# Retention states in a hybrid encoder layer: one 128x128 product per chunk, or one 64x64 product per head in the array's column halves

## The chip, the cores and the metric

The kernel runs on one core of a Trainium2 chip. The metric is the time of one execution on the device in microseconds; each kernel is run several times, and the median is taken. The engines of the core work side by side, each in the order of its own instructions: TensorE (PE: matmuls and transpositions; its weight loads are listed apart as PEld), VectorE (DVE), ScalarE (ACT), GpSimd (POOL) and SyncE (SP, which issues most of the DMAs). They wait for each other by semaphores. Matmuls write to PSUM, which has eight banks of 128 partitions x 2 KB; VectorE and ScalarE copy results out of it.

## The reference, cut to what matters

One encoder layer on a sequence of 1024 rows of width 1024, in float32. An input projection feeds two groups of heads side by side: eight heads of retention in both directions, and eight heads of windowed attention. Their outputs are projected, normalised, and go through a gated feed-forward part. The change concerns retention alone. Its recurrence goes over 8 chunks of 128 rows, head dimension 64, and for each head and each direction:

```python
scores = jnp.einsum('bhncd,bhnsd->bhncs', q, k) * decay_in[None, :, None]
y_inner = jnp.einsum('bhncs,bhnse->bhnce', scores, v)
kv = jnp.einsum('bhnsd,bhnse->bhnde', k * k_decay[None, :, None, :, None], v)

def step(state, kv_n):
    return state * chunk_decay[None, :, None, None] + kv_n, state

_, r_prev = lax.scan(step, jnp.zeros((b, h, d, d), q.dtype), jnp.moveaxis(kv, 2, 0))
y_cross = jnp.einsum('bhncd,bhnde->bhnce', q * q_decay[None, :, None, :, None], r_prev)
```

`kv` is a 64x64 product per head, chunk and direction; the scan turns these products into the states that precede each chunk. The sum of both directions is normalised per head and multiplied by a gate.

## The kernel before

**Tiling.** Two heads make a pair and lie side by side in 128 partitions or columns; there are four pairs (`NPAIR`). Large products run as three fp32r matmuls of 128x512 (`mm3`, L77 to L79), from operands split into a high and a low part (`split`, L71 and L72). Small products of retention and attention run in plain float32, which TensorE executes as two matmul instructions per product; a transposition is one.

**Order of the work.** In the stage around the change the instructions of TensorE stand in the order in which the program writes them. The other engines' queues are ordered by the framework from the program and its own estimate of time. `run(steps, total)` goes through a list: an entry is a step of retention or attention, or `F`, which stands for a share of `total` (48) filler units taken from a queue; a unit is one `mm3`, three matmuls of the input projections. The units also count time: a step can be put off to a later unit (`later`, for the scaling of scores), and side work is tied to units (`side`, which splits later weights into high and low parts and stores them to DRAM: L570 to L572, with sums before it at L606 or L631).

**PSUM.** There are four roles of two banks each: "mm" for the projections, "s" for scores, "t" for transpositions and for the states' products, "o" for outputs. A bank can be written again when its last reader is done.

**Retention of one pair** (class `Retention`, L374): `keys` (K, L384) transposes chunks of the keys into a "t" bank (L390) and multiplies them by the decays of both directions into `kdec` (L393); before, four calls with two chunks each. `kv` (C, L399) multiplies `kdec` of both heads with the values of both heads, 128x128 per chunk and direction (L404), 14 products per pair, since the last chunk of each direction leads to no state; of each product only the two 64x64 blocks on the diagonal are wanted, and the copy out of PSUM multiplies the rest by zero with a mask (`C_BD`, L408). `scan` (L413) runs the recurrence on VectorE in 12 steps of 128x128 (L416 and L419). `scores` (Q, L422) multiplies queries and keys in row halves of the array (L429), then VectorE applies the decays (L432) and makes the decayed queries `qq` (L435). `out` (Y, L438) adds the products with the scores and with the states in an "o" bank (L449 to L461). `norm` (N) normalises; `turn` (X, L483) transposes the result (L488) into a "t" bank, and ScalarE copies it out as `y` (L489).

**Attention of the same pair** stands between these steps: `scores(n)` (sco, L502) writes two "s" banks (L517, L518), VectorE reads them with a running maximum (L519, L521), ScalarE takes the exponential (L523) and, `LAG` units later, scales it (L529); `turn(n)` (trn, L534) transposes it into two "t" banks (L541), which ScalarE copies out as `ptr` (L543); `values(n)` (val, L546) multiplies them with the values in column halves of the array (L553).

In pair 0 retention stands with fillers alone; in pairs 1 to 3 both groups of heads share the list. `gate(i)` (L684, L685) multiplies the finished `y` by Silu of the gate's projection; its fillers fall into pair 3 and after it.

Of the kernel before, what the change touches and what calls it, by code (L numbers as in the profile page):

```python
# [11 lines left out]
AF = mybir.ActivationFunctionType  # L12
ALU = mybir.AluOpType
# [3 lines left out]
P = 128  # L17
# [3 lines left out]
NT = S // P  # L21
# [15 lines left out]
C_KF, C_KB, C_MH, C_TWO, C_BD = 1024, 1025, 1026, 1027, 1028  # L37
# [5 lines left out]
def layer(tc, xT, xn, w_first, w_mt, w_rv, w_out, w_pg, w_pe, pT, w_gu, w_dn,  # L43
          consts, dec_b, dec_c, sink, gng, lnp, out):
    nc = tc.nc
    act, dve, pool, pe, sp = nc.scalar, nc.vector, nc.gpsimd, nc.tensor, nc.sync
# [12 lines left out]
    def nm(s):  # L59
        uid[0] += 1  # L60
        return f"{s}{uid[0]}"

    def bank(tag, shape=(P, HF)):
        tag = ROLE[tag]
        return ps.tile(list(shape), F32, tag=tag, bufs=NB[tag], name=nm("b" + tag))
# [55 lines left out]
    def a_tile(shape, name, tag=None, dt=F32):  # L121

        turnA[0] += tag is None
        return big.tile(list(shape), dt, tag=tag or f"A{turnA[0] % 2}", bufs=4, name=nm(name))
# [8 lines left out]
    def bt(shape, tag, bufs=None, dt=F32):  # L133
        return bpool.tile(list(shape), dt, tag=tag, bufs=bufs, name=nm(tag))
# [15 lines left out]
    with tc.manual_schedule(engines={mybir.EngineType.DVE, mybir.EngineType.SP}):  # L150
        for kt in range(KT):
            r = xraw[kt]
# [36 lines left out]
    cst = cp.tile([P, C_W], F32, name="cst")  # L189
# [27 lines left out]
    kd = cp.tile([P, 2, 8], F32, name="kd")  # L217
# [35 lines left out]
    for h in range(2):  # L253
        sl = slice(h * HF, (h + 1) * HF)
        b = st[1, h]
        for g in range(2):
            a = slice(64 * g, 64 * g + 64)
# [14 lines left out]
    def take(k):  # L272
        for _ in range(min(k, len(queue))):
            queue.pop(0)()
            ticks[0] += 1
            for what in (later, side):
                for x in [x for x in what if x[0] <= ticks[0]]:
                    what.remove(x)
                    x[1]()
# [49 lines left out]
    rv = bt([P, NT, HF], "rv")  # L329

    def proj_rv():
# [12 lines left out]
        def step(t, kt):  # L344
            if kt == 0:
                hold["b"] = bank("mm")
            b = hold["b"]
            c = slice(t * P, (t + 1) * P)
            mm3(b, xs[kt][:, 0, c], xs[kt][:, 1, c], wr[kt][:, 0, :], wr[kt][:, 1, :], kt == 0, kt == KT - 1)
            if kt == KT - 1:  # L350
                if t % 2:
                    dve.tensor_copy(rv[:, t, :], b)
                else:
                    act.activation(rv[:, t, :], b, AF.Copy)

        return [lambda kt=kt: load(kt) for kt in range(KT)], \
            [lambda t=t, kt=kt: step(t, kt) for t in range(NT) for kt in range(KT)]

    decays = {}

    def decay_q(i):
# [12 lines left out]
    class Retention:  # L374


        def __init__(self, i, y):
            self.i, self.y = i, y
            self.rk, self.rq, _ = pairs[i]
            self.A = [bt([P, NT - 1, P], f"kv{d}") for d in range(2)]  # L380
            self.kdec, self.pt, self.qq, self.ym, self.ready = {}, {}, {}, {}, set()
            self.qd, self.dt = decays[i]

        def keys(self, q):  # L384

            i = self.i
            tb = bank("t", (P, 2, P))
            for j in range(2):
                n = 2 * q + j
                pe.transpose(tb[:, j, :], self.rk[:, n * P:(n + 1) * P], ident)  # L390
            kdec = self.kdec[q] = bt([P, 2, 2, P], "kdec")
            for d in range(2):
                dve.tensor_tensor(  # L393
                    kdec[:, d].rearrange("p n (h e) -> p n h e", h=2),
                    tb.rearrange("p n (h e) -> p n h e", h=2),
                    kd[:, d, 2 * i:2 * i + 2].unsqueeze(1).unsqueeze(3).to_broadcast([P, 2, 2, 64]),
                    ALU.mult)

        def kv(self, q):  # L399
            b = bank("t", (P, 2, 2, P))  # L400
            js = [[j for j in range(2) if 2 * q + j != (7, 0)[d]] for d in range(2)]
            for d in range(2):
                for j in js[d]:
                    pe.matmul(b[:, d, j, :], self.kdec[q][:, d, j, :], rv[:, 2 * q + j, self.i * P:(self.i + 1) * P],  # L404
                              start=True, stop=True)
            for d in range(2):
                j0, j1 = js[d][0], js[d][-1] + 1
                dve.tensor_tensor(  # L408
                    self.A[d][:, 2 * q + j0 - d:2 * q + j1 - d, :].rearrange("p n (h e) -> p n h e", h=2),
                    b[:, d, j0:j1, :].rearrange("p n (h e) -> p n h e", h=2),  # L410
                    cst[:, C_BD:C_BD + 2].unsqueeze(1).unsqueeze(3).to_broadcast([P, j1 - j0, 2, 64]), ALU.mult)

        def scan(self):  # L413
            i, A = self.i, self.A
# [273 lines left out]
    def run(steps, total):  # L688

        shares = steps.count(None)  # L690
        done = n = 0
        for f in steps:
            if f is None:
                n += 1
                take(total * n // shares - done)
                done = total * n // shares
            else:
                f[0](*f[1:])

    F = None  # L700
    with tc.manual_schedule(engines={mybir.EngineType.PE}):
        enqueue([mtile(0, ev_av), proj_rv(), *project(1), *project(2), *project(3), gate(0), gate(1), gate(2), gate(3)])

        spare = [bt([P, S], "rkq", 3), bt([P, S], "aq", 3, F32R)]
        twin = lambda t: t.rearrange("p (a b) -> p a b", a=2)
        ops = [twin(spare[1]), a_tile([P, 2, HF], "pro", "A0", F32R)]
        side.extend(presplit_out(0, ops, 17.5, 4))
        side.extend(presplit_out(1, ops, 44, 4, spare[:1]))
        a = Attention(0, ytile(1))
        sco, trn, val = (lambda n: (a.scores, n)), (lambda n: (a.turn, n)), (lambda n: (a.values, n))  # L710
        run([F, F, sco(0), F, sco(1), F], 16)
        run([F, (av_turn, 0), (av_turn, 1), F, trn(0), sco(2), F, trn(1), sco(3), F, val(0), val(1), trn(2), sco(4), F,
             trn(3), sco(5), F, val(2), val(3), trn(4), sco(6), F, trn(5), sco(7), F, val(4), val(5), trn(6), (decay_q, 0),
             F, trn(7), (decay_k, 0, 0), F, val(6), val(7), (decay_k, 0, 1), F], 64)
        assert not side and not later
        y0 = ytile(0)
        side.extend(presplit_gate())
        r = Retention(0, y0)
        K, C, N = (lambda q: (r.keys, q)), (lambda q: (r.kv, q)), (lambda q: (r.norm, q))
        Q, X = (lambda q: (r.scores, q)), (lambda q: (r.turn, q))  # L720
        Y = lambda hh, k: (r.out, hh, (2 * k, 2 * k + 1))
        run([K(0), F, C(0), K(1), Q(0), F, C(1), K(2), F, C(2), K(3), F, C(3), (r.scan,), F, F, Y(0, 0), Y(0, 1), N(0), Q(1),
             F, (decay_q, 1), F, (decay_k, 1, 0), Y(1, 0), Y(1, 1), N(1), (decay_k, 1, 1), F, F], 48)
        V = []
        for i in range(1, NPAIR):
            assert i == 1 or not side, len(side)
            X0, X1 = X(0), X(1)
            r = Retention(i, ytile(2 * i))
            a = Attention(i, ytile(2 * i + 1))
            if i == 2:  # L730
                late = [ytile(6), ytile(7)]
                op = twin(late[1].bitcast(F32R))
                side.extend(presplit_out(2, [op], 2, 3.5, late[:1]))
                side.extend(presplit_small(0, op, 30) + presplit_small(1, op, 38))
            elif i == 3:
                op = twin(bt([P, S], "aq", 3, F32R))
                side.extend(presplit_out(3, [op], 4, 3.5, [bt([P, S], "rkq", 3)]))
                side.extend(presplit_small(2, op, 32) + presplit_small(3, op, 40))
            G = [(f, i + 1, *x) for f, x in ((decay_q, ()), (decay_k, (0,)), (decay_k, (1,)))] if i + 1 < NPAIR else \
                [(lambda: None,)] * 3  # L740
            run([*V, K(0), X0, Q(0), F, C(0), K(1), sco(0), F, C(1), K(2), sco(1), F, trn(0), sco(2), F, C(2), K(3), F,
                 trn(1), sco(3), F, C(3), X1, (r.scan,), val(0), val(1), F, trn(2), sco(4), F, trn(3), sco(5), F,
                 Y(0, 0), Y(0, 1), N(0), val(2), val(3), Q(1), F, G[0], trn(4), sco(6), F, G[1], Y(1, 0), trn(5), sco(7), F,
                 G[2], val(4), val(5), Y(1, 1), N(1), F, trn(6), F, trn(7), F], 48)
            V = [val(6), val(7)]
        run([F, X(0), X(1), *V, F, F], 16)
# [35 lines left out]
    def four(k):  # L782
        return [bank(t) for t in sets[k]]
# [289 lines left out]
    pt = {t: load_p(t) for t in range(2)}  # L1073
# [37 lines left out]
    pt = {t: load_p(t) for t in range(2)}  # L1111
    Y = four("a")
# [161 lines left out]
    n = 0  # L1274
# [304 lines left out]
    with tc.manual_schedule(engines={ET.PE, ET.DVE, ET.Activation, ET.Pool, ET.SP}):  # L1579
        ahead(2, 4)  # L1580
        for k in range(NG):
# [5 lines left out]
            j = k + 1 - NG  # L1587
# [104 lines left out]
```

## Time and profile before

| | |
|---|---|
| Median of 3 runs | 1200.38 us (1199.83 to 1201.25) |
| Span of the profiled execution, first to last instruction | 1197.3 us |
| TensorE busy | 1180.5 us, 99% of the span |
| VectorE busy | 772.9 us, 65% |
| ScalarE busy | 542.2 us, 45% |
| GpSimd busy | 364.6 us, 30% |
| Mean granted TensorE clock | 0.998 |

Of the profiled execution the profile gives the span; the time of the whole execution is known from the timed runs. A row of a group of instructions reads: source line, engine, operation, output <- inputs by the program's names, shape, count | busy time in us, mean duration in ns | idle time of the engine just before them, and what ended it. In the timeline a row gives the start and the length in us, and at the end in brackets the idle time before it with what ended it. Durations of matmuls overlap, so what one costs is read from the distance between two starts.

### The profile page before, as it was taken

To read this page: it belongs to the slowest core of one execution; us is meant where nothing else is said; L and a number is where in the kernel's file an instruction comes from. 1 tells how busy PE (TensorE), PEld (TensorE's weight loads), DVE (VectorE), ACT (ScalarE), POOL (GpSimd) and SP (SyncE) were. 2 spreads that over 40 slices of the span, in tenths; PEclk is the share of its full clock that TensorE was granted. 3 is DMA by queue.
4 is the path that set the end of the run, shared out by engine and by line. 5 is a ranking of instruction groups with operands and counts; after the bars stand their busy time and mean duration, and the time that the engine had idled before them with its cause. 6 is when DMAs were issued, how large, how long until landed. Compare 5 with 4: busy or idle time off the path is not lost.

```text
span 1197.3 us, 16664 instructions
## 1 busy us (share of the span) xinstructions
PE 1180.5 (99%) x5892; PEld 984.1 (82%) x5892; DVE 772.9 (65%) x1346; ACT 542.2 (45%) x1046; POOL 364.6 (30%) x342
## 2 busy tenths in 40 slices
PE   9999999999999999999999999999999999999996
PEld 7888888888888888788888888888888888888885
DVE  5554788867767788947744554545554566774677
ACT  5566238576786257203333332333322325552453
POOL 2001020203010022002756465564746342134232
PEclk9999999999999999999999999999999999999999
DMA  7336635434336864666233311332123169999977
GB/s 255 111 132 218 248 116 212 161 121 161 122 124 236 319 234 168 238 221 209 88 123 132 132 64 68 132 132 100 77 88 132 71 203 307 368 269 207 260 173 208
DMA packets 78098, 207.80 MB, mean 174 GB/s; under 512 B 9024, under 2 KB 13248, under 8 KB 78016
## 3 DMA queue, kind: packets, MB, share of 16 engines
q1 hardware_dynamic: 69376, 189.98, 44.3%
q0 software_dynamic: 8640, 16.78, 8.0%
q8 instruction: 46, 0.75, 0.2%
q14 instruction: 36, 0.29, 0.1%
HBM read 139.35 MB, written 62.13 MB: 168 GB/s over the span
## 4 chain that ended last, share of the span: by engine, by line
PE 86%; DVE 4%; issue 3%; DMA 3%; POOL 2%; ACT 1%; DVEq 0%; SPq 0%; POOLq 0%; ACTq 0%
PE bmm L77 6%; PE bmm L79 6%; PE bmm L78 5%; PE bs L763 5%; PE bt L763 5%; PE bt L764 5%; PE bt L765 5%; PE bs L764 5%; PE bs L765 5%; PE bmm L763 4%; PE bmm L765 4%; PE bmm L764 4%; PE bo L763 4%; PE bo L765 4%; PE bo L764 4%
## 5 line engine op out<-in xcount | busy, mean ns | idle before, releaser
L77 PE MATMUL bmm<-H,w 128*128 128x512 f32 x240 | 96.7, 403 | 0.1
L79 PE MATMUL bmm<-H,w 128*128 128x512 f32 x240 | 94.1, 392 | 0.0
L78 PE MATMUL bmm<-H,w 128*128 128x512 f32 x240 | 93.8, 391 | 0.0
L1161 POOL TENSOR_TENSOR H<-ln 128x512 f32<-128x512 f32 x22 | 28.8, 1311 | 180.5 <-DMA ln<-in_w_gu 180.5
L1191 POOL TENSOR_TENSOR ev<-ev 128x512 f32<-128x512 f32 x33 | 54.9, 1665 | 91.1 <-DVE ev L1206 40.0
L72 DVE TENSOR_TENSOR w<-H,w 128x512 fp32r<-128x512 f32 x44 | 40.2, 914 | 62.6 <-ACT w L71 62.6
L72 DVE TENSOR_TENSOR w<-raw,w 128x512 fp32r<-128x512 f32 x56 | 45.6, 816 | 45.6 <-ACT w L71 45.3
L514 POOL COPY sc<-skb 128x1 f32<-128x1 f32 x64 | 12.9, 206 | 184.8 <-PE bt L541 145.9
L1189 ACT ACTIVATE ev<-ev 128x512 f32<-128x512 f32 x33 | 20.9, 632 | 102.7 <-DVE ev L1206 102.7
L1195 POOL TENSOR_TENSOR ev<-ev,ev 128x512 f32<-128x512 f32 x44 | 62.7, 1436 | 2.6
L72 DVE TENSOR_TENSOR u<-H,u 128x512 fp32r<-128x512 f32 x47 | 37.2, 792 | 39.8 <-ACT u L71 39.4
L77 PEld LDWEIGHTS bmm<-H,w 128*128 128x128 f32 x240 | 45.1, 188 | 9.9 <-ACT H L71 0.7
L79 PEld LDWEIGHTS bmm<-H,w 128*128 128x128 f32 x240 | 45.0, 188 | 9.9
L78 PEld LDWEIGHTS bmm<-H,w 128*128 128x128 f32 x240 | 45.2, 188 | 7.8
L71 ACT ACTIVATE u<-H 128x512 fp32r<-128x512 f32 x47 | 29.6, 631 | 45.1 <-PE bt L765 11.1
L523 ACT ACTIVATE sc<-sc,st 128x385 f32<-128x385 f32 (+1 forms) x64 | 37.2, 583 | 25.1 <-DVE st L521 25.1
L519 DVE CUSTOM_DVE_ANT_0 sc<-cst,bs,skb 128x384 f32<-128x384 f32 (+1 forms) x64 | 34.9, 576 | 17.0 <-PE bs L518 16.5
L71 ACT ACTIVATE w<-raw 128x512 fp32r<-128x512 f32 x56 | 34.7, 624 | 17.5 <-PE bo L79 5.5
L475 POOL TENSOR_TENSOR sm<-sm,cst 128x8 f32<-128x8 f32 x8 | 15.0, 1875 | 86.8 <-DVE sm L474 86.8
L874 POOL TENSOR_TENSOR stt<-stt,cst 128x1 f32<-128x1 f32 x8 | 12.1, 1516 | 91.0 <-DVE stt L873 91.0
L1165 POOL TENSOR_TENSOR H<-raw,H 128x512 f32<-128x512 f32 x22 | 37.8, 1717 | 0.0
L71 ACT ACTIVATE w<-H 128x512 fp32r<-128x512 f32 x44 | 27.4, 622 | 22.0 <-PE bs L765 6.3
(802 smaller groups left out, 3825.0 us busy)
## 6 DMA issues: line engine op xcount, KB each, us to landing
ad<-ev SPq DMA_DIRECT2D x33, 512.0 KB, 2.7
pgd<-pro SPq DMA_DIRECT2D x28, 512.0 KB, 2.8
raw<-in_w_gu SPq DMA_DIRECT2D x22, 512.0 KB, 4.3
ln<-in_w_gu SPq DMA_DIRECT2D x22, 512.0 KB, 3.5
raw<-ad SPq DMA_DIRECT2D x40, 256.0 KB, 5.8
ln<-ad SPq DMA_DIRECT2D x37, 256.0 KB, 6.7
H<-in_w_dn SPq DMA_DIRECT2D x33, 256.0 KB, 7.6
wod<-aq SPq DMA_DIRECT2D x15, 512.0 KB, 2.7
```

What stands on the lines that cost most here:

```text
L71: act.activation(hi, raw, AF.Copy)
L72: dve.tensor_tensor(lo, raw, hi.bitcast(F32), ALU.subtract)
L77: pe.matmul(o, lh, rh, start=start, stop=False)
L78: pe.matmul(o, lh, rl, start=False, stop=False)
L79: recent[0] = pe.matmul(o, ll, rh, start=False, stop=stop).ins.name
L523: act.activation(sc[g][:, :nk + 1], sc[g][:, :nk + 1], AF.Exp, bias=st_[:, 1, j, g:g + 1], accum_out=st_[:, 2, j, g:g + 1])
L763: pe.matmul(o, lh, rh, start=start, stop=False, skip_group_check=True)
L764: pe.matmul(o, lh, rl, start=False, stop=False, skip_group_check=True)
L765: pe.matmul(o, ll, rh, start=False, stop=stop, skip_group_check=True)
L1165: pool.tensor_tensor(s[3], a(0, 1), s[0], ALU.subtract)
L1191: pool.tensor_tensor(c[:, 1, :], c[:, 0, :], c[:, 1, :], ALU.mult)
L1195: pool.tensor_tensor(self.ev[dst][:, 0, :], left, right, op)
```

## The change

The two state tiles are allocated once and their blocks off the diagonal filled with zero by GpSimd. `keys` takes four chunks per call, two calls per pair, and keeps `kdec` in the buffers of `qq` and `pt`, which the scores fill later. `kv` is one call per pair: for each chunk, direction and head a product of 64 columns of `kdec` with 64 columns of the values, the two heads in the two column halves of the array, all of a half sequence in one "t" bank. Each bank is copied into the diagonal blocks by VectorE for the first head and by ScalarE for the second. In the lists of steps, K stands twice, C is replaced by the one call of `kv`, directly before Q(0); in pairs 1 to 3 the scan comes earlier, X1 stands directly ahead of trn(1), and there are 17 shares of filler instead of 15, so a share is 2 or 3 units instead of 3 or 4.

```diff
+    states = [bt([P, NT - 1, P], f"kv{d}") for d in range(2)]
+    for d in range(2):
+        for h in range(2):
+            pool.memset(states[d][64 * h:64 * h + 64, :, 64 * (1 - h):64 * (1 - h) + 64], 0.0)
...
-            self.A = [bt([P, NT - 1, P], f"kv{d}") for d in range(2)]
+            self.A = states
...
         def keys(self, q):
-            tb = bank("t", (P, 2, P))
-            for j in range(2):
-                n = 2 * q + j
+            tb = bank("t", (P, 4, P))
+            for j in range(4):
+                n = 4 * q + j
                 pe.transpose(tb[:, j, :], self.rk[:, n * P:(n + 1) * P], ident)
-            kdec = self.kdec[q] = bt([P, 2, 2, P], "kdec")
+            kdec = self.kdec[q] = bt([P, 2, 4, P], ("qq", "pt")[q])
...
-        def kv(self, q):
-            b = bank("t", (P, 2, 2, P))
-            js = [[j for j in range(2) if 2 * q + j != (7, 0)[d]] for d in range(2)]
-            for d in range(2):
-                for j in js[d]:
-                    pe.matmul(b[:, d, j, :], self.kdec[q][:, d, j, :], rv[:, 2 * q + j, self.i * P:(self.i + 1) * P],
-                              start=True, stop=True)
-            for d in range(2):
-                j0, j1 = js[d][0], js[d][-1] + 1
-                dve.tensor_tensor(
-                    self.A[d][:, 2 * q + j0 - d:2 * q + j1 - d, :].rearrange("p n (h e) -> p n h e", h=2),
-                    b[:, d, j0:j1, :].rearrange("p n (h e) -> p n h e", h=2),
-                    cst[:, C_BD:C_BD + 2].unsqueeze(1).unsqueeze(3).to_broadcast([P, j1 - j0, 2, 64]), ALU.mult)
+        def kv(self):
+
+            for q in range(2):
+                b = bank("t", (P, 2, 4, 64))
+                js = [[j for j in range(4) if 4 * q + j != (7, 0)[d]] for d in range(2)]
+                for d in range(2):
+                    for j in js[d]:
+                        for h in range(2):
+                            a = slice(64 * h, 64 * h + 64)
+                            v = self.i * P + 64 * h
+                            pe.matmul(b[a, d, j, :], self.kdec[q][:, d, j, a], rv[:, 4 * q + j, v:v + 64],
+                                      start=True, stop=True)
+                for d in range(2):
+                    j0, j1 = js[d][0], js[d][-1] + 1
+                    for h in range(2):
+                        a = slice(64 * h, 64 * h + 64)
+                        to = self.A[d][a, 4 * q + j0 - d:4 * q + j1 - d, a]
+                        if h:
+                            act.activation(to, b[a, d, j0:j1, :], AF.Copy)
+                        else:
+                            dve.tensor_copy(to, b[a, d, j0:j1, :])
...
-        run([K(0), F, C(0), K(1), Q(0), F, C(1), K(2), F, C(2), K(3), F, C(3), (r.scan,), F, F, Y(0, 0), Y(0, 1), N(0), Q(1),
+        run([K(0), F, K(1), F, F, (r.kv,), Q(0), F, (r.scan,), F, F, Y(0, 0), Y(0, 1), N(0), Q(1),
              F, (decay_q, 1), F, (decay_k, 1, 0), Y(1, 0), Y(1, 1), N(1), (decay_k, 1, 1), F, F], 48)
...
-            run([*V, K(0), X0, Q(0), F, C(0), K(1), sco(0), F, C(1), K(2), sco(1), F, trn(0), sco(2), F, C(2), K(3), F,
-                 trn(1), sco(3), F, C(3), X1, (r.scan,), val(0), val(1), F, trn(2), sco(4), F, trn(3), sco(5), F,
+            run([*V, K(0), X0, F, K(1), F, sco(0), F, (r.kv,), Q(0), F, sco(1), F, trn(0), sco(2), (r.scan,), F, X1, trn(1),
+                 sco(3), F, F, val(0), val(1), F, trn(2), sco(4), F, trn(3), sco(5), F,
                  Y(0, 0), Y(0, 1), N(0), val(2), val(3), Q(1), F, G[0], trn(4), sco(6), F, G[1], Y(1, 0), trn(5), sco(7), F,
                  G[2], val(4), val(5), Y(1, 1), N(1), F, trn(6), F, trn(7), F], 48)
```

More of the change, by code (lines that the diff above doesn't have):

```diff
@@ L395, in keys @@
                     tb.rearrange("p n (h e) -> p n h e", h=2),
-                    kd[:, d, 2 * i:2 * i + 2].unsqueeze(1).unsqueeze(3).to_broadcast([P, 2, 2, 64]),
+                    kd[:, d, 2 * i:2 * i + 2].unsqueeze(1).unsqueeze(3).to_broadcast([P, 4, 2, 64]),
                     ALU.mult)
-        def kv(self, q):
-            b = bank("t", (P, 2, 2, P))
-            js = [[j for j in range(2) if 2 * q + j != (7, 0)[d]] for d in range(2)]
-            for d in range(2):
-                for j in js[d]:
-                    pe.matmul(b[:, d, j, :], self.kdec[q][:, d, j, :], rv[:, 2 * q + j, self.i * P:(self.i + 1) * P],
-                              start=True, stop=True)
-            for d in range(2):
-                j0, j1 = js[d][0], js[d][-1] + 1
-                dve.tensor_tensor(
-                    self.A[d][:, 2 * q + j0 - d:2 * q + j1 - d, :].rearrange("p n (h e) -> p n h e", h=2),
-                    b[:, d, j0:j1, :].rearrange("p n (h e) -> p n h e", h=2),
-                    cst[:, C_BD:C_BD + 2].unsqueeze(1).unsqueeze(3).to_broadcast([P, j1 - j0, 2, 64]), ALU.mult)
+        def kv(self):
[18 more added lines that the diff above has]
+                            dve.tensor_copy(to, b[a, d, j0:j1, :])
         def scan(self):
@@ L718, in layer @@
         r = Retention(0, y0)
-        K, C, N = (lambda q: (r.keys, q)), (lambda q: (r.kv, q)), (lambda q: (r.norm, q))
+        K, N = (lambda q: (r.keys, q)), (lambda q: (r.norm, q))
         Q, X = (lambda q: (r.scores, q)), (lambda q: (r.turn, q))
         Y = lambda hh, k: (r.out, hh, (2 * k, 2 * k + 1))
-        run([K(0), F, C(0), K(1), Q(0), F, C(1), K(2), F, C(2), K(3), F, C(3), (r.scan,), F, F, Y(0, 0), Y(0, 1), N(0), Q(1),
+        run([K(0), F, K(1), F, F, (r.kv,), Q(0), F, (r.scan,), F, F, Y(0, 0), Y(0, 1), N(0), Q(1),
              F, (decay_q, 1), F, (decay_k, 1, 0), Y(1, 0), Y(1, 1), N(1), (decay_k, 1, 1), F, F], 48)
```

## The prediction

> **What bounds the kernel now.** I read the page first, then who waited for whom on TensorE, then single sections of TensorE's timeline, then the queues of VectorE and ScalarE around the retention and attention steps.
>
> ```profile
> span 1197.3 us, 16664 instructions
> PE 1180.5 (99%) x5892; PEld 984.1 (82%) x5892; DVE 772.9 (65%) x1346; ACT 542.2 (45%) x1046; POOL 364.6 (30%) x342
> ```
>
> TensorE is busy for 1180.5 of 1197.3 us. Its order is written out by hand, so it can be neither reordered nor filled: time taken out of its stream comes off the end, time that it waits is added to the end. The timed runs (median 1200.38) lie 3.1 us above the profile's span; I take that offset as fixed and add the changes of the span to the median. The waits that are there already, from the list of waits of TensorE:
>
> ```profile
> PE bo L763 <- DVE sg L1053: 2.1, 1, 2.1
> PE bt L404 <- ACT ptr L543: 1.6, 1, 1.6
> PE bs L517 <- DVE pt L432: 1.3, 1, 1.3
> ```
>
> The last two are in the stage that is changed: a product of C waited for a "t" bank that ScalarE had not yet copied out, a score of attention for an "s" bank that VectorE had not yet multiplied out: 2.9 us. They show what can hold TensorE here: two banks per role, and queues in order behind them.
>
> **Part 1: the products themselves.** The timeline of TensorE, a section of C, one of attention's values (column halves already), and one of the retention output:
>
> ```profile
> 183.20 1.05 PE L404 MATMUL bt<-rv,kdec 128*128 128x128 f32 x8
> 184.09 0.38 PE L390 MATMUL bt<-cst,rkq 128*128 128x128 f32 x2
> ...
> 191.29 0.49 PE L488 MATMUL bt<-cst,ym 128*128 128x128 f32 x3
> 191.71 1.31 PE L553 MATMUL bo<-ptr,av 128*64 128x128 f32 x20
> 192.95 0.50 PE L77 MATMUL bmm<-H,w 128*128 128x512 f32 x1
> ...
> 145.69 0.56 PE L449 MATMUL bo<-rv,pt 128*128 128x64 f32 x4
> 146.08 0.44 PE L456 MATMUL bo<-kv,qq 128*128 128x128 f32 x2
> ```
>
> Starts, not durations, price a matmul, since they overlap. Eight matmuls of C take 184.09 - 183.20 = 0.89 us, 0.111 each. An f32 product is two such instructions, so a pair's 14 products are 28 steps, 3.11 us. After the change 14 products for each of two heads are 56 instructions, but two run side by side, again 28 steps. What is a step now? The four of L449 move only 64 columns and still take 0.39 us: three at 0.112 and one, whose weights were there already, at 0.39 - 3 x 0.112 = 0.055. So moving 64 columns costs 0.055 us, and a load of 128 weight columns is what makes 0.11. The weight loads:
>
> ```profile
> L553 PEld LDWEIGHTS bo<-ptr,av x352: 132/137/137, 79.8 to 366.5; 128*64 128x64 f32 x176
> L404 PEld LDWEIGHTS bt<-rv,kdec x112: 186/192/192, 122.9 to 320.9; 128*128 128x128 f32 x112
> ```
>
> A load of 64 columns is 192 - 137 = 55 ns shorter than one of 128, so half a load is about 0.055 us too. Do the load of one half and the move of the same half overlap? In the values section 20 instructions, 10 steps side by side, take 192.95 - 191.71 = 1.24 us; a step that moves 128 columns (0.11) after a load that was not hidden (0.055) would be 0.165, 1.65 us in all. So they overlap, and a step of the new section is the larger of 0.055 and 0.055; I take 0.058, with bounds 0.055 and 0.111 (nothing gained). Saving: 28 x (0.111 - 0.058) = 1.48 us a pair, 5.9 us for four.
>
> Here a page speaks against the change. The Trainium skill, TensorE: Matmul & The Clock Gate, section Part 3: Packing small matmuls, says that a weight load overlaps with matmuls in flight only when its row group differs; two column halves share all rows. By that rule load and move would add up to 0.11 and the saving would be none. The 1.24 us above disagree with it for the values' column halves; the new section's moves are half as long, and no row here shows that form. It comes back as a rival.
>
> Changing the form of the array costs: from the third transposition of L488 (191.29 + 2 x 0.11 = 191.51) to the first of L553 it is 0.20 instead of 0.11 us. The scores that follow are row halves and had both their switches before; new is one switch per pair, from full array to column halves: +0.09 x 4 = +0.4 us. The eight transpositions of K are the same eight, in two sections.
>
> **Part 2: what leaves and enters the other queues.** VectorE, its groups, and two rows of its timeline for the distance of starts:
>
> ```profile
> L408 DVE TENSOR_TENSOR kv<-bt,cst 128x256 f32<-128x256 f32 x24 | 9.5, 415 | 7.3 <-PE bt L404 7.3
> L416 DVE SCALAR_TENSOR_TENSOR kv<-kv,cd 128x128 f32<-128x128 f32 x24 | 8.3, 345 | 0.1
> L432 DVE TENSOR_TENSOR pt<-bs,dt 128x512 f32<-128x512 f32 x16 | 10.4, 682 | 0.1
> L519 DVE CUSTOM_DVE_ANT_0 sc<-cst,bs,skb 128x384 f32<-128x384 f32 x48 | 27.8, 610 | 13.6 <-PE bs L518 13.1 <-ACT ptr L543 0.4
> ```
> ```profile
> 236.09 1.29 DVE L432 TENSOR_TENSOR pt<-bs,dt 128x512 f32<-128x512 f32 x2
> 237.30 0.68 DVE L72 TENSOR_TENSOR w<-raw,w 128x512 fp32r<-128x512 f32 x1
> ```
>
> Two products of 512 columns take 237.30 - 236.09 = 1.21 us, so in a dense row the next one starts some 0.08 us before the duration of 0.68 is over. In the same way I take 0.34 for a copy, 0.61 for any step of 512 columns (sums, splits, qq, pt), 0.53 for a score; a scan step hangs on the one before and keeps its 0.35. kv: eight masked copies of VectorE become four copies there and four on ScalarE (64 partitions, about 0.34 to 0.4 each by L408). Off the path by themselves; but the built order lets ScalarE's copy of a bank wait for VectorE's and VectorE's next for ScalarE's, so the two hand a bank back and forth. Eight small multiplications of K become four of twice the width, no gain and no loss. kdec in the buffers of qq and pt makes their next writers wait for kv's products, which TensorE does first anyway: nothing. The four zero fills on GpSimd lie long before their first reader: nothing. DMAs are moved by none of this.
>
> In the built order the scan in pair 0 must now end between kv and the first output, in 3 shares of filler. VectorE has from kv's first bank on 4 copies, 9 steps of 512 columns and 12 steps of the scan, 1.4 + 5.5 + 4.2 = 11.1, with the hand-backs 11.7 us; TensorE has the second half of kv, the scores (8 steps of 0.11 and the switches around them) and 42 filler matmuls (0.23 each, below), 0.8 + 1.2 + 9.6 = 11.6. On the edge: +0.1, between 0 and 1.5.
>
> **Part 3: the wait that comes.** The new row of steps in pairs 1 to 3 is "trn(0), sco(2), scan, F, X1, trn(1)". X1 takes one "t" bank and trn(1) two, one behind the other, and there are two. So the second half of trn(1) starts only when ScalarE has copied X1's y out (L489). Before, at most two such tiles stood between two fillers, and even that once cost 1.6 us. In the built order ScalarE has between sco(1) and that y: two exponentials of sco(1), two copies of trn(0), two scalings, two exponentials of sco(2), a presplit copy (L570), the rk or rq copy (L228, 512 columns too, taken at L570's 0.5), then y. The timeline of ScalarE prices them:
>
> ```profile
> 190.33 0.62 ACT L523 ACTIVATE sc<-sc,st 128x385 f32<-128x385 f32 x1 [0.30 <-DVE st L521]
> ...
> 190.95 0.60 ACT L523 ACTIVATE sc<-sc,st 128x385 f32<-128x385 f32 x1
> ...
> 191.55 0.61 ACT L570 ACTIVATE pro<-pre 128x512 fp32r<-128x512 f32 x1
> 192.07 1.11 ACT L529 ACTIVATE sc<-sc,st 128x384 f32<-128x384 f32 x2
> 193.08 0.67 ACT L489 ACTIVATE y<-bt,gn 128x512 f32<-128x512 f32 x1
> ...
> 306.72 1.28 ACT L684 ACT_TABLE_LOAD   x1
> 308.01 0.60 ACT L684 ACTIVATE sq<-bmm 128x512 f32<-128x512 f32 x1
> ...
> 312.67 0.63 ACT L543 ACTIVATE ptr<-bt 128x256 f32<-128x256 f32 x2
> ```
>
> and TensorE's its side:
>
> ```profile
> 187.08 0.82 PE L541 MATMUL bt<-cst,sc 128*128 128x128 f32 x6
> 187.65 0.42 PE L517 MATMUL bs<-k,aq 128*128 128x384 f32 x1
> ...
> 188.43 0.40 PE L77 MATMUL bmm<-H,w 128*128 128x512 f32 x1
> 188.67 0.39 PE L78 MATMUL bmm<-H,w 128*128 128x512 f32 x1
> 188.89 0.39 PE L79 MATMUL bmm<-H,w 128*128 128x512 f32 x1
> ```
>
> ScalarE: 1.2 + 0.5 + 1.0 + 1.2 + 0.5 + 0.5 + 0.7 = 5.6 us from the moment that the first exponential may start. TensorE from the end of sco(1), if nothing held it: 9 filler matmuls 2.1 (0.23 each by the last three rows), trn(0) 0.4 (0.1 a transposition by L541), sco(2) 0.8 (188.43 - 187.65), 6 fillers 1.4, X1 0.4, the first half of trn(1) 0.3: 5.4. So TensorE waits by the time from the end of sco(1) to the step of VectorE that lets the exponentials start (L521), and 0.2 more. That step has its place behind these, in the built order: pair 1, after the second pt product, an add, two scan steps, a score, a split, a score, a split; pair 2, five scan steps, a split, two scores, a scan step; pair 3, a split, a scan step, two scores, a scan step. Counted from the start of what follows pt: 3.6, 3.8 and 2.4 us. Where does VectorE stand then? From kv's first bank on it has 4 copies, 2 qq and 2 pt products and about 0.6 of handing back, 4.4 us; TensorE comes to the second half of sco(1), which needs the bank that the second pt product frees, after 0.8 + 1.2 + 2.1 + 0.4 = 4.5. So both arrive together, sco(1) ends at 4.9, and L521 comes at 4.4 + 3.6, 3.8 or 2.4: late by 3.1, 3.3 and 1.9 us.
>
> Pair 3 has more in ScalarE's queue: gate(0) has its copies there, so its exponentials and the second Silu each need a table load (1.28 each), with a Silu for the rk copy, a second presplit copy (0.5), and the scalings wait 0.6 for VectorE: 2 x 1.28 + 0.5 + 0.6 = 3.7 us more. With the 0.2 and 0.1 for semaphores the waits are 3.4, 3.6 and 5.9, together 12.9 us. The bounds: if nothing were queued on either engine, y would still come a score, L521, two exponentials, L570, L228 and L489 after sco(2), 0.7 + 0.1 + 1.2 + 0.5 + 0.5 + 0.7 = 3.7, where TensorE needs 1.4 + 0.4 + 0.3 = 2.1: 1.6 in pairs 1 and 2, 2.9 with a table load in pair 3, 6.1 in all; upwards 1 us a pair more.
>
> Two small ones: in pair 1 VectorE reaches kv 1.3 us late (the gate's presplit steps are queued ahead), so sco(1) waits 1.3, between 0 and 1.5; K(1) now stands one filler behind X0 and takes its bank, whose copy is third in ScalarE's queue at 0.6 each: 0.2 in pairs 2 and 3, 0.4.
>
> The two old waits (2.9) go, as their places do: C and the score after Q(0) stand elsewhere.
>
> **Sum:** 1200.4 - 5.9 + 0.4 - 2.9 + 0.1 + 12.9 + 1.3 + 0.4 = 1206.7 us.
>
> **The rivals.** *ScalarE and VectorE keep up* (faster): if they have worked off their queues when sco(2) is done, only the floor of 6.1 us is left and the small waits do not come: 1200.4 - 5.9 + 0.4 - 2.9 + 6.1 = 1198.1. It decides where the new waits sum to 6.0 us. Engines that are so far ahead would also shorten TensorE's old wait for L1053, 2.1 us at most: 1196.0; I put it at 1197. For it: VectorE has idle time in the stage (7.3 us ahead of L408 alone). Against it: that idle time sits at other places of its order, and the old stream lost 1.6 us with one bank less in demand. *The halves do not overlap* (the page's rule): every step stays at 0.111, 5.9 us are not gained: 1212.6. Against it the 1.24 us of the values. *Later waits give back*: TensorE's 2.1 us for L1053 is on another engine; if that engine runs ahead while TensorE waits, 1204.6; it lies in the forecast's own range. *Half of the lag*: VectorE earlier by 1.6 us in each pair: 1201.9.
>
> **How the numbers follow.** The forecast (waits as summed) 0.66, its own range 1203 to 1210 (1 us a pair, and sco(1) from 0 to 1.5); halves without overlap 0.10; half of the lag 0.08; both keep up 0.16. A measurement of this kernel tells about 0.2% from no change, 2.4 us: 1198.0 to 1202.8. Faster: most of the last, 0.14. Same: its rest, the half lag and the foot of the forecast, 0.12. Slower: 0.74. The range 1198 to 1212.6 leaves out 0.14 below and about 0.05 above.
>
> **What would show it.** Right: 56 instructions of kv a pair starting two by two each 0.06 us; among TensorE's waits new rows of trn's matmuls on ScalarE's y, one of 3 to 6 us in each of pairs 1 to 3, the third the longest; X1 waiting for ptr in pair 3; the rows of L404 and L517 gone. Wrong: kv's steps at 0.11; or trn's waits under 1 us, with ScalarE idle before y. The forecast falls if the exponentials of sco(2) end before TensorE has done X1.

## The result and the profile after

| | before | changed |
|---|---|---|
| median, runs made together (6 each) | 1201.09 us (1199.83 to 1204.78) | 1212.7 us (1211.56 to 1216.89) |
| ratio, changed to before | | 1.0101, 95% interval 1.0083 to 1.0119 |
| the profiled execution: its time, its span | span 1197.3 us | 1211.71 us, span 1209.7 us |
| mean granted TensorE clock in it | 0.998 | 0.993 |

The changed kernel is 1.0% slower. The forecast of 1206.7 us had the sign and about half of the loss; the measured median lies 0.1 us above the upper end of its range. The page and the list of TensorE's waits (us in total, times, longest):

```profile
span 1209.7 us, 16880 instructions
...
PE 1181.1 (98%) x6004; PEld 979.2 (81%) x6004; DVE 766.7 (63%) x1314; ACT 548.2 (45%) x1062; POOL 369.1 (31%) x346
```
```profile
PE bt L553 <- ACT y L501: 8.9, 3, 3.5
PE bmm L77 <- DVE rkq L231: 2.3, 2, 1.2
PE bo L775 <- DVE sg L1065: 2.1, 1, 2.1
PE bs L775 <- DVE acc L1403: 2.0, 1, 2.0
PE bt L500 <- ACT ptr L555: 1.8, 1, 1.8
...
PE bt L394 <- ACT y L501: 0.5, 1, 0.5
...
PE bs L529 <- DVE pt L444: 0.2, 1, 0.2
```

Lines behind the change are 12 higher than before (L541 is L553, L543 is L555, L489 is L501, L763 is L775). The rows of C's wait and of the score behind Q(0) are gone from their places (the 0.2 of L529 stand in pair 3); trn(1)'s three waits for y are new and the largest; so are two waits of filler matmuls (L77) for VectorE's copy of rq (L231), which the prediction does not have.

To tell the gains and losses apart I measure one stretch in each kernel: from the first transposition of K in pair 0 to the first product of gate and up, both read off TensorE's timeline. Before it is 374.43 - 120.1 = 254.3 us, in the changed kernel 383.86 - 120.4 = 263.5: **9.2 us longer**. By pairs, from K(0) to the next K(0): pair 0 is 1.3 us shorter, pairs 1 to 3 are 2.3, 3.4 and 4.9 us longer. The other 3.2 us of the two spans' 12.4 lie outside; they come back below.

**The products** took what was forecast. TensorE's timeline in pair 0:

```profile
130.61 0.39 PE L79 MATMUL bmm<-H,w 128*128 128x512 f32 x1
130.93 1.03 PE L413 MATMUL bt<-rv,qq 128*64 128x64 f32 x28
131.79 0.99 PE L413 MATMUL bt<-rv,pt 128*64 128x64 f32 x28
132.71 1.16 PE L441 MATMUL bs<-rkq,rkq 64*128 64x128 f32 x16
```

56 instructions take 132.71 - 130.93 = 1.78 us with the switch to the scores; inside, two start together every 0.0585 us. The rule of the Trainium skill (TensorE: Matmul & The Clock Gate, Part 3: Packing small matmuls) that a weight load overlaps only when the row group differs would have made it 3.1 us; this trace does not bear it out for two column halves of 64 columns.

**The wait of trn(1)** in pair 1, on TensorE and in the queues of VectorE and ScalarE:

```profile
179.16 0.33 PE L530 MATMUL bs<-kz,aq 128*128 128x384 f32 x1
...
184.12 0.66 PE L500 MATMUL bt<-cst,ym 128*128 128x128 f32 x4
184.94 0.55 PE L553 MATMUL bt<-cst,sc 128*128 128x128 f32 x3 [0.16 <-ACT sc L541]
188.21 0.55 PE L553 MATMUL bt<-cst,sc 128*128 128x128 f32 x3 [2.73 <-ACT y L501]
```
```profile
182.16 0.15 DVE L533 TENSOR_SCALAR st<-st 128x2 f32<-128x2 f32 x1
```
```profile
182.34 0.62 ACT L535 ACTIVATE sc<-sc,st 128x385 f32<-128x385 f32 x1 [1.21 <-DVE st L533]
...
187.49 0.67 ACT L501 ACTIVATE y<-bt,gn 128x512 f32<-128x512 f32 x1
```

The last score of sco(1) is done at 179.16 + 0.33 = 179.49; VectorE comes to the step that lets its exponentials start 2.7 us later, and ScalarE needs 187.49 + 0.67 - 182.34 = 5.8 us from there to the end of y (5.6 forecast). X1 and the first half of trn(1) fill the two "t" banks by 185.5; the second half starts at 188.21. In pair 3 two table loads stand in ScalarE's queue besides, one ahead of sco(1)'s exponentials and one between those of sco(2) and y:

```profile
316.53 1.28 ACT L535 ACT_TABLE_LOAD   x1 [0.31 <-DVE st L533]
...
322.63 1.28 ACT L696 ACT_TABLE_LOAD   x1
```

**What was not forecast: half speed behind a wait.** Pair 3, where the wait is longest, in TensorE's timeline, and windows of it and of the gate stage (length | busy time and instructions of five engines | granted clock, DMA share, GB/s):

```profile
325.67 0.90 PE L553 MATMUL bt<-cst,sc 128*128 128x128 f32 x3 [3.48 <-ACT y L501]
...
327.65 0.63 PE L77 MATMUL bmm<-H,w 128*128 128x512 f32 x1
328.08 0.63 PE L78 MATMUL bmm<-H,w 128*128 128x512 f32 x1
...
329.73 0.39 PE L79 MATMUL bmm<-H,w 128*128 128x512 f32 x1
329.96 0.39 PE L77 MATMUL bmm<-H,w 128*128 128x512 f32 x1
```
```profile
325.50:329.50 4.00, 3.83 (x12) 3.44 (x13) 3.11 (x9) 2.11 (x5) 0.55 (x1) 0.50 0.48 184
...
500.20:503.60 3.40, 3.40 (x10) 2.71 (x9) 3.40 (x4) 0.00 (x0) 0.00 (x0) 0.52 1.03 363
```

For some 4 us after the wait the granted clock is 0.50, and filler matmuls start 328.08 - 327.65 = 0.43 us apart instead of 0.23. Against the same instructions behind the wait of pair 2, which run at full speed, that costs 1.8 us: 0.9 on fillers, as much on the transpositions and scores ahead of them. The same happened in the gate stage, after the old wait of 2.1 us (1.6 us lost).

### The profile page after: what moved, and what is told of

Its sections match the earlier page's. It is cut to its first block, busy times and chain, and to the rows that moved or that the text cites. A ratio compares the mean times of both kernels' runs of the same rounds, so it can differ in the third digit from the quotient of the medians.

```text
span 1209.7 us, 16880 instructions
## 1 busy us (share of the span) xinstructions
PE 1181.1 (98%) x6004; PEld 979.2 (81%) x6004; DVE 766.7 (63%) x1314; ACT 548.2 (45%) x1062; POOL 369.1 (31%) x346
## 4 chain that ended last, share of the span: by engine, by line
PE 85%; DVE 6%; ACT 3%; DMA 3%; issue 2%; POOL 1%; DVEq 0%; POOLq 0%; ACTq 0%
PE bt L777 5%; PE bt L776 5%; PE bt L775 5%; PE bs L775 5%; PE bs L777 5%; PE bs L776 5%; PE bmm L77 5%; PE bmm L78 5%; PE bmm L79 5%; PE bmm L775 5%; PE bmm L776 5%; PE bmm L777 5%; PE bo L776 4%; PE bo L775 4%; PE bo L777 4%
## 5 line engine op out<-in xcount | busy, mean ns | idle before, releaser
L77 PE MATMUL bmm<-H,w 128*128 128x512 f32 x240 | 97.8, 407 | 2.3 <-DVE rkq L231 2.3
L526 POOL COPY sc<-skb 128x1 f32<-128x1 f32 x64 | 17.1, 279 | 201.3 <-PE bt L553 185.4
L77 PEld LDWEIGHTS bmm<-H,w 128*128 128x128 f32 x240 | 45.5, 189 | 13.1 <-DVE rkq L231 3.2
```

What stands on the lines that cost most here:

```text
L77: pe.matmul(o, lh, rh, start=start, stop=False)
```

## The experiments

One table for all; the texts follow. The stretch is compared with that of the first profile of before (254.3 us); ratios are to the kernel before on the same chips. The code below is shown shortened.

| run | stretch, us | median, us | ratio (95% interval) |
|---|---|---|---|
| changed | +9.2 | 1212.7 | 1.0101 (1.0083 to 1.0119) |
| changed, again | +14.6 | 1213.54 | 1.0101 (1.0085 to 1.0118) |
| X1 later | +0.4 | 1200.81 | 0.9989 (0.9975 to 1.0004) |
| form alone | -1.6 | 1200.81 | 0.9992 (0.9977 to 1.0006) |
| order alone | +15.8 | 1215.78 | 1.0123 (1.0096 to 1.0149) |
| copies on VectorE alone | +10.3 | 1212.72 | 1.0089 (1.0062 to 1.0116) |
| X1 later, Q(1) earlier | -2.7 | 1197.91 | 0.9975 (0.9966 to 0.9985) |
| X1 later, trn(1) later | -1.4 | 1197.42 | 0.997 (0.9957 to 0.9983) |
| all moves | -6.2 | 1194.39 | 0.9948 (0.9935 to 0.996) |
| before, again | -0.6 | 1199.85 (one run) | |
| changed, Q(1) earlier | +8.5 | 1206.6 | 1.0043 (1.003 to 1.0056) |

**X1 later.** Is it three "t" tiles in a row?

```diff
-  ... trn(0), sco(2), (r.scan,), F, X1, trn(1), sco(3), F, F, val(0), val(1), ...
+  ... trn(0), sco(2), (r.scan,), F, trn(1), sco(3), F, X1, F, val(0), val(1), ...
```

> The changed kernel with one step moved: X1 stands behind sco(3) and one share of filler instead of ahead of trn(1). Theory (three t tiles in a row for two banks): the three rows of trn(1) waiting for ScalarE's y (2.9, 2.9 and 3.65 us) and X1's wait for ptr in pair 3 (1.9) go, about 0.6 comes back as short waits of X1 for the copies of trn(1); the 2.6 us for the copies of rq stay: 1212.7 - 10.8 = 1202. If the half-speed filler matmuls behind the third wait (0.9 us) go too: 1201. Rival (ScalarE and VectorE are late at this place whatever stands there): waits of about 3 us a pair come up again at X1 or val(0), 1207 to 1211.

The list of waits of this kernel:

```profile
PE bmm L77 <- DVE rkq L231: 2.3, 2, 1.2
...
PE bt L553 <- ACT ptr L555: 1.7, 1, 1.7
...
PE bt L553 <- ACT sc L541: 1.3, 2, 0.8
...
PE bt L500 <- ACT ptr L555: 0.6, 1, 0.6
PE bt L394 <- ACT y L501: 0.5, 1, 0.5
```

The rows for y at trn(1) are gone and the stretch is 8.8 us shorter than in the changed kernel. trn(1) still waits 3.0 us, for a bank (ptr) once and for its scaled scores (L541) twice: ScalarE is late by itself. So the place of X1 made most of the wait. The stretch has no half speed any more, and the median, 1200.81, is near the 1201 expected for that case.

**Form alone.** The kernel before, with each head's product in its column half, and the masked product of VectorE reading each 64 columns twice.

```diff
-            b = bank("t", (P, 2, 2, P))
+            b = bank("t", (P, 2, 2, 64))
...
-                    pe.matmul(b[:, d, j, :], self.kdec[q][:, d, j, :], rv[:, 2 * q + j, self.i * P:(self.i + 1) * P], ...)
+                    for h in range(2):
+                        a, v = slice(64 * h, 64 * h + 64), self.i * P + 64 * h
+                        pe.matmul(b[a, d, j, :], self.kdec[q][:, d, j, a], rv[:, 2 * q + j, v:v + 64], ...)
...
-                    b[:, d, j0:j1, :].rearrange("p n (h e) -> p n h e", h=2),
+                    b[:, d, j0:j1, :].unsqueeze(2).to_broadcast([P, j1 - j0, 2, 64]),
```

> The kernel before, its order unchanged, with the new form of the products alone: two heads side by side in the column halves, four sections a pair as before, and VectorE's masked product reads each 64 columns twice (as many and as wide VectorE steps as before, none on ScalarE). Theory (a step of a column-half pair is 0.0585 us instead of 0.111): 28 x 0.0525 x 4 = 5.9 us less on TensorE, and 16 sections with a switch in and out, some 0.14 together, 2.2 more: 1201.1 - 3.7 = 1197.4, with the two old waits (1.6 and 1.3) still there. Rival (short sections cost a bare start each, or the waits for banks grow by what the products gain): 1200 to 1201.

The rival was nearer: a ratio of 0.9992, where 3.7 us would be 0.9969, outside the interval. A section of six steps in this kernel's timeline:

```profile
123.31 0.39 PE L79 MATMUL bmm<-H,w 128*128 128x512 f32 x1
123.63 0.57 PE L407 MATMUL bt<-rv,kdec 128*64 128x64 f32 x12
124.13 0.44 PE L390 MATMUL bt<-cst,rkq 128*128 128x128 f32 x2
124.50 1.16 PE L432 MATMUL bs<-rkq,rkq 64*128 64x128 f32 x16
```

From the filler to the transpositions it is 124.13 - 123.31 = 0.82 us, where six full-width steps would be 0.23 + 6 x 0.11 = 0.89: of 6 x 0.0525 = 0.32 us, 0.25 go into the switch in (0.32 instead of 0.23 to the first start), a first step of 0.11 and the way out. The two transpositions behind it take 124.50 - 124.13 = 0.37 us to the scores' start instead of 0.11 + 0.20. So the form pays in one long section a pair, as the change has it: 1.3 us in pair 0, which has no waits, against 0.2 in the same pair here (46.35 us instead of 46.56, K(0) to K(0)) and 0.4 a pair over the stretch.

**Order alone.** The changed kernel with full-width products and masks.

```diff
-            for q in range(2):
-                b = bank("t", (P, 2, 4, 64))
+            for q in range(4):
+                b = bank("t", (P, 2, 2, P))
...
+                        pe.matmul(b[:, d, j, :], self.kdec[q // 2][:, d, 2 * (q % 2) + j, :], rv[...128 columns...], ...)
```

> The changed kernel with its order, its keys and its buffers, but the full-width products of the kernel before with VectorE's masked copies, all in one section of four banks. Theory (the form gains 5.9 us in the changed kernel, its order costs): 1212.7 + 5.5 = 1218, and up to 2 more where the third and fourth bank of a section wait for VectorE. If the longer section lets VectorE catch up by 1 us a pair, 1215. Rival (the form's gain never reached the end, since what TensorE gained it waited for later): 1212 to 1213.

TensorE's timeline, and two of its waits:

```profile
175.44 1.72 PE L410 MATMUL bt<-rv,qq 128*128 128x128 f32 x14
178.17 1.80 PE L410 MATMUL bt<-rv,pt 128*128 128x128 f32 x14 [1.01 <-DVE kv L414]
```
```profile
PE bt L547 <- ACT y L495: 7.8, 3, 3.5
...
PE bt L410 <- DVE kv L414: 1.9, 3, 1.0
```

The stretch is 6.6 us longer than with the new form: 1.9 of new waits for VectorE's copies, 1.1 less at trn(1) and 0.5 less at X1, some 0.9 more at half speed behind trn(1), which leaves some 5 us for the form, near the 5.5 of the first theory. So the form's gain reaches the end of the stretch. The median rose by only 3 us, to 1215.78, near the 1215 named for the case that VectorE catches up, and the two kernels' intervals overlap (1.0096 to 1.0149 and 1.0083 to 1.0119): the medians alone do not tell the two theories apart.

**Copies on VectorE alone.**

```diff
-                    for h in range(2):
-                        ...
-                        if h: act.activation(to, b[a, d, j0:j1, :], AF.Copy)
-                        else: dve.tensor_copy(to, b[a, d, j0:j1, :])
+                    dve.tensor_tensor(<both heads' blocks>, b[:, d, j0:j1, :] read twice, <mask C_BD>, ALU.mult)
```

> The changed kernel, with the copies of the states on VectorE alone: for each bank and direction one masked product that reads each 64 columns twice (up to 512 columns, about 0.6 us), instead of a copy on VectorE and one on ScalarE that hand the bank back and forth. Theory (VectorE's lag behind sco(1) sets the wait of trn(1)): VectorE's own time is 4 x 0.6 = 2.4 us against 4 x 0.34 and about 0.6 to 1 of handing back, so the lag and the waits change by less than 0.5 us a pair: 1211 to 1214. Rival (the handing back is what makes it late): 1 us a pair less, 1209.

```profile
PE bt L550 <- ACT y L498: 8.8, 3, 3.5
...
PE bt L497 <- ACT ptr L552: 2.3, 1, 2.3
```

The median is that of the changed kernel; the stretch is 1.1 us longer, X1's wait 0.5 of it. The handing of a bank between VectorE and ScalarE is not what makes them late.

**X1 later and Q(1) earlier; X1 and trn(1) later; all moves.** From the kernel with X1 later:

```diff
-  Y(0, 0), Y(0, 1), N(0), val(2), val(3), Q(1), F, ...
+  Y(0, 0), Y(0, 1), N(0), Q(1), val(2), val(3), F, ...          # Q(1) earlier
-  (r.scan,), F, trn(1), sco(3), F, X1, F, val(0), ...
+  (r.scan,), F, F, trn(1), sco(3), F, X1, val(0), ...           # trn(1) later
-  K(0), X0, F, K(1), F, sco(0), F, (r.kv,), ...
+  K(0), X0, F, sco(0), K(1), F, F, (r.kv,), ...                 # only in "all moves"
```

> As the run with X1 later, and Q(1) ahead of val(2) and val(3) instead of behind them, so that VectorE's products pt can start 1.5 us earlier. Theory (the two waits of filler matmuls for the copy of rq, 1.3 us each in pairs 1 and 2, come from that copy's place in VectorE's queue behind pt and the norm's steps): both shrink by about 1 us or go: 2 us less than the run with X1 later. Rival (VectorE is full at this place, so the copy comes as late): no change.

> As the run with X1 later, and trn(1) with sco(3) one more share of filler (2.1 us) behind the scan; X1 keeps its place behind the share after sco(3). Theory (ScalarE's chain of exponentials, copies and scalings is late by a fixed time behind sco(1)): trn(1)'s waits of 1.0, 0.6 and 1.8 us go, X1's 0.8 stays or grows to 1: 3 us less than the run with X1 later. Rival (what waits later gives the time back or the chain is late by whatever TensorE does): under 1 us less.

> Both moves above together, and sco(0) ahead of K(1), so that the copy of y out of X0's bank has 0.8 us more. If the waits are independent: 1.0 + 0.6 + 1.8 + 2 of 2.6 + 0.6 for K(1) = 6 us less than the run with X1 later, 5 to 6 less than the kernel before. If one wait is only handed on to the next: 0 to 3 less.

VectorE's queue at Q(1) of pair 1, first the changed kernel, then the one with Q(1) earlier:

```profile
210.81 0.68 DVE L444 TENSOR_TENSOR pt<-bs,dt 128x512 f32<-128x512 f32 x1
211.41 0.68 DVE L231 COPY rkq<-bmm 128x512 f32<-128x512 f32 x1
```
```profile
209.38 0.69 DVE L231 COPY rkq<-bmm 128x512 f32<-128x512 f32 x1
209.99 0.68 DVE L444 TENSOR_TENSOR pt<-bs,dt 128x512 f32<-128x512 f32 x1
```

With 17 shares Q(1) stands behind 31 filler units (48 x 11 / 17), before behind 28 (48 x 9 / 15); the tile of rq ends at unit 32, so its copy falls among VectorE's work of Q(1) and N(0), and the next filler needs its bank. The moves of Q(1) show that this place makes the waits; that the number of shares brought it there is read from the lists, and the old number was not tried. With Q(1) earlier the copy stands ahead of pt and both waits are gone: 3.1 us of the stretch against "X1 later" (K(1)'s wait was 0.5 us shorter too), 2.9 us of the median. trn(1) later took 1.8 and 3.4 us, all moves 6.5 and 6.4 us; measured against the kernel before on the same chips it is 1.7, 2.3 and 4.9 us (ratios times 1201). For trn(1) later 3 us were expected: its waits went down from 3.0 to 0.6 us, but X1's for ptr grew from 0.6 to 2.5. The waits were in the main separate losses, most of which can be taken away together. What is left in the last kernel:

```profile
PE bt L500 <- ACT ptr L555: 2.4, 2, 2.1
...
PE bt L553 <- ACT y L501: 0.6, 1, 0.6
```

X1 now waits for ScalarE in trn(1)'s place, mostly in pair 3 with its table loads. This kernel is 0.5% faster than the one before (0.9948, 0.9935 to 0.996) and beats both.

**Before, again.**

> The kernel before, unchanged, profiled once more. In its first profile no filler matmul after the 2.3 us wait of the gate and up stage ran at half speed; the changed kernel and three of its variants and relatives show 5 to 8 matmuls 0.43 us apart some 3 us after that same wait, 1.0 to 1.6 us in all. If this comes and goes from run to run, it can be here too: span 1197.3, or about 1198.8 with it. If it hangs on the order of the changed kernels, it is not here.

Windows around and behind the wait for the gate's products, in the first profile of before and in this one:

```profile
487.00:492.00 5.00, 2.88 (x14) 2.03 (x13) 5.00 (x6) 1.06 (x1) 0.00 (x0) 1.00 1.01 368
492.00:510.00 18.00, 18.00 (x81) 14.92 (x80) 17.32 (x19) 4.25 (x4) 0.00 (x0) 1.00 0.63 221
```
```profile
491.00:494.50 3.50, 3.50 (x10) 2.70 (x9) 3.50 (x5) 0.00 (x0) 0.00 (x0) 0.52 1.02 382
```

The same kernel, the same wait of 2.1 us, with and without the stretch at half speed: it comes and goes. So those 1.6 us of the changed kernel's first profile are not due to the change.

**Changed, again; changed with Q(1) earlier** (the same move of Q(1) as above, X1 where the change put it).

> The changed kernel, unchanged, once more. In its first profile the stretch from K(0) of pair 0 to the first product of gate and up is 9.2 us longer than before; 3.2 us more were lost outside it. Theory (what was lost outside comes and goes from run to run and the kernel before has as much of it on average): the stretch is again 9 to 9.5 us longer, the losses outside differ from 3.2, and the median is 9 to 10 us above that of the kernel before. Rival (the losses outside belong to the change): 12 us above it, the same rows outside.

> The changed kernel with Q(1) ahead of val(2) and val(3), and X1 where the change put it. Theory (the waits for the copy of rq, 2.3 us in two rows, are a loss of their own that the prediction left out): they go, the rows of trn(1) stay at 8.9 us, 2.5 us less than the changed kernel. Rival (time that TensorE doesn't lose there it loses at the next of trn(1)'s waits): under 1 us less, with longer rows of trn(1).

The repeat has the same waits to 0.2 us in the stretch, yet the stretch is 5.4 us longer. The windows that follow the same wait of pair 2, in the first profile of the changed kernel and in the repeat, and last one of the repeat behind the wait of pair 1:

```profile
256.50:264.50 8.00, 8.00 (x51) 6.49 (x50) 4.63 (x12) 4.61 (x11) 0.19 (x1) 1.00 0.37 123
```
```profile
258.90:266.90 8.00, 8.00 (x32) 6.49 (x32) 4.72 (x12) 4.67 (x11) 0.18 (x1) 0.66 0.29 86
190.40:192.60 2.20, 2.20 (x7) 1.72 (x6) 2.18 (x9) 0.74 (x3) 0.00 (x0) 0.50 0.07 28
```

In the same 8 us TensorE did 51 matmuls in the one and 32 in the other. In the repeat all three waits of trn(1) are followed by half speed, 22 fillers at 0.2 us more each and the transpositions and scores around them: 1.6, 2.8 and 2.5 us in the three pairs, some 7 us, against 1.8 in the first profile. Without it the two stretches are 7.4 and 7.7 us longer than before. My theory of 9 to 10 us was wrong, the median is again 12 us above; the rival, that the losses outside belong to the change, holds only for one of them: the wait for acc (L1403) near the end was 2.0 and 2.4 us in the two profiles of the changed kernel and 1.9 with the copies on VectorE, 1.1 and none in the two of before, and 0.2 or none in all others; in the repeat half speed came behind it too (granted clock 0.50 from 1189.4 to 1192.8). Whether that is the change or the moment at which the end falls stays open.

With Q(1) earlier the changed kernel lost both waits for rq, trn(1)'s rows stayed at 8.9 us, and half speed came after two of the three, 2.6 and 2.4 us: without it the stretch is 3.6 us longer than before, 3.8 less than in the changed kernel, over the 2.5 of the theory (K(1)'s wait, 0.5, and that of a score in pair 3, 0.4, went as well). The median fell by 7 us, more than that; the difference of the clock (0.993 or 0.994 in its runs, 0.989 to 0.994 in those of the changed kernel) and the wait for acc, which this profile does not have, go the same way, but how much each gave was not measured apart.

## Why the forecast had the sign and half the size

The steps in the order of the prediction, in the stretch; measured as the distance of two starts beyond what the same pair of lines takes elsewhere, which is 0.1 to 0.2 us more than a wait's row.

| step | forecast, us | measured, us |
|---|---|---|
| products and switches | -5.9 + 0.4 = -5.5 | 4 x -1.33 (pair 0, without waits) = -5.3 |
| old waits gone | -2.9 | -3.8 (with 0.4 of values waiting for ptr in pair 2) |
| scan in pair 0 | +0.1 | 0 |
| trn(1) and X1, pairs 1, 2, 3 | 3.4 + 3.6 + 5.9 = 12.9 | 3.4 + 3.2 + 5.7 = 12.3 |
| sco(1) in pair 1 | +1.3 | +0.2 |
| K(1) | +0.4 | +0.6 (pair 2 alone) |
| copy of rq at Q(1), pairs 1 and 2 | none | +2.6 |
| half speed behind the waits | none | +1.8 in the first profile, about 7 in the repeat |
| others (a score in pair 3; rest not traced) | none | +0.8 |
| sum | +6.3 | +9.2 in the first profile |

*Part 1* was right: a step of 0.0585 us against 0.058 forecast, halves overlap, and the switch costs what was put. *Part 3* was right in mechanism and size: L533 came 2.7 us behind the end of sco(1) (3.1 forecast), ScalarE's chain took 5.8 us (5.6), and the third wait is the longest because of the two table loads; X1 waits for ptr in pair 3, as named. That most of the wait comes from X1's place was shown by moving it. The *rival that ScalarE and VectorE keep up* fell with the same rows, *halves do not overlap* with those of L413. That its number, 1212.6, is close to the result is chance.

**The steps that failed** are two terms missing from the sum. First, Part 2 followed VectorE's queue only through kv, the scan and the scores behind them, and not to Q(1), though the list of shares that moves Q(1) from unit 28 to 31 stands in the change: 2.6 us. sco(1)'s 1.3 us, which TensorE lost only 0.2 of, is a mis-sized term in the other direction. Second, the sum took a wait of TensorE at its own length ("time that it waits is added to the end") and put nothing down for what follows it: 1.8 us in the first profile's stretch, about 7 in the repeat's. The traces show that the matmuls after it may run at half speed; in the changed kernel three waits of 2.9 to 3.7 us stand in the stretch where before there was none over 1.8. Runs of one kernel show the same: before has, in its 54 runs beside the experiments, spans of 1196.3 to 1199.9 us at a mean clock of 0.998, and 1202.7 and 1203.1 at 0.994; the changed kernel's 12 runs have 0.989 to 0.994, and 1208.4 us at 0.994. With gains and waits alone (7.4 and 7.7 us in the stretch) it would have ended near 1201.1 + 7.5 = 1208.6 us, an estimate that leaves the share of half speed that before has as it is; half speed behind the new waits, and perhaps the wait for acc, made it 1212.7. The later wait for L1053 (L1065 now) stayed at 2.1 us in both, so nothing was given back there.

## What to carry to other kernels

Count, for every place where the order changes, how many tiles of one role follow each other without other work between them, against the banks of that role: the third tile waits for the slowest copy queued ahead of the first. Follow the filler's own evacuations through the reordered queue too, since a different number of shares moves all of them. And price a wait of TensorE of 2.3 us or more at more than its length, while a new form of small products is worth its gain only if a section is long enough to pay for the way in and out.

## What the runs showed of the hardware

After a wait of TensorE the granted clock can be 0.50 for some 3 to 6 us, and matmuls of 512 columns then start 0.43 us apart instead of 0.23. The traces' record of the clock has 17 such stretches between the first 10 us and the last matmul of the twelve profiles, each 3.4 or 6.8 us long, and none of them stands apart from a wait of 2.3 us or more: they start between 3.0 us before the wait's end and 1.5 us behind it. What falls into the wait itself costs nothing, so the price varies from run to run. With the waits measured as distances of starts, 5 of 5 waits of 3.65 us were followed by it, 4 of 8 of 2.8 to 2.9 us, 8 of 15 of 2.3 to 2.6 us, none of 9 of 1.8 to 2.2 us (short waits that a longer one follows at once are left out). The Trainium skill (TensorE: Matmul & The Clock Gate, Part 1: The HAM clock gate) has a free-running window of about 3.4 us behind the clock: that the stretches last one or two such windows, and come and go behind the same wait, agrees with it. Its advice in the section Why this matters for your kernels, to keep idle gaps under about 3 us, was not enough here: 2.3 us had the same effect in half the cases. What decides a single case was not tried.
